# A decoder block with product-key experts: splits, one-hots and stored tiles issued earlier, and a second of four one-hots on VectorE

## The chip, the cores and the metric

The kernel runs on one core of one Trainium2 chip (trn2). The metric is the device time of one execution in microseconds (us). The kernel before took 1837.16 us, the median of three runs that lie between 1837.00 and 1837.48 us. Where engines are named: PE is TensorE, ACT is ScalarE, DVE is VectorE, POOL is GpSimd, and SP is the queue of SyncE, from which most transfers are started.

## The reference

One decoder block: 512 tokens of width 1024 behind 16 meta tokens, a mixer of stick-breaking attention and gated linear attention, then a mixer of 16384 single-neuron experts, of which each of 8 heads picks 16 by product keys, and a last norm. The change lies wholly in the second mixer:

```python
def peer_ffn(hn, w_peer_q, sub_keys1, sub_keys2, expert_u, expert_v):
    q = (t @ w_peer_q).reshape(T, PEER_HEADS, 2, PEER_HALF)
    s1 = jnp.einsum('thd,hkd->thk', q[:, :, 0], sub_keys1)
    s2 = jnp.einsum('thd,hkd->thk', q[:, :, 1], sub_keys2)
    v1, i1 = lax.top_k(s1, PEER_TOPK)
    v2, i2 = lax.top_k(s2, PEER_TOPK)
    cand = (v1[..., :, None] + v2[..., None, :])      # 256 sums per head
    sc, pos = lax.top_k(cand, PEER_TOPK)
    eidx = ...                                        # i1 * 128 + i2 of the 16 best
    gates = jax.nn.softmax(sc, axis=-1)
    act = jax.nn.gelu(jnp.einsum('nkd,nd->nk', expert_u[e], xt), approximate=False)
    return jnp.einsum('nk,nkd->nd', g * act, expert_v[e])
```

Everything is float32.

## The kernel before, in words

The 512 tokens are four blocks of 128. For block 3 (`GATHER`) the kernel fetches the chosen rows of `expert_u` and `expert_v` by indirect transfers. For blocks 0 to 2 (`DENSE`, 384 tokens) it multiplies with all 16384 experts and weights each activation by a matrix of gates that is zero where an expert wasn't chosen.

The experts are handled in 128 rows of 128. A **U row** (`u_row`, lines 832 to 842) loads one 512 KB tile `uf` of `expert_ut`, splits it into a high and a low part (`hilo`, line 174: ACT makes `uh` at line 175, DVE makes `ul` at line 176), multiplies both with the split tokens in 24 products `pj` of 128x384 (lines 180 to 182), and takes the Gelu into `ge` on ACT (line 842). A **V row** (`v_operands` and `v_block`, lines 847 to 870) loads a tile of `expert_v` into the same ring of `uf` buffers, splits it, multiplies `ge` with the gates `gt` (DVE, line 859), splits the result into `wh` and `wl`, and adds 18 products of 128x512 into six banks `acc`. Two rows are a **pair** and share one `ge` tile.

The gate matrix has to be made first. `topk(blk)` finds the 16 experts per head on DVE (lines 640 to 718). `spread(blk)` (line 744) then turns the lists of one block into the matrix: for each **group** of four tokens, `B` is a one-hot of the second key (four Abs at line 786 and a Relu at line 787 on ACT, or one comparison at line 781 on DVE), `Am` is the gated one-hot of the first key (POOL, line 789, from `ohu` and `ohl`, which DVE makes once for four groups), four float32 products `sx` join them (line 793, eight TensorE instructions in the profile), and ACT copies the bank into `st` (line 794). After four groups `st` goes to `Gd` in device memory. A block has 32 groups; `B` and `Am` have three buffers each.

The program has three stretches here. In the **look stretch** (lines 892 to 901) a `Queue` holds topk and spread of the blocks in turn; after each U row it writes out as much of them as a budget of 5.04 us (4.2 * 1.2) pays for at the costs they yield, and the finished U rows are stored in `Ad`. This takes 22 pairs. In the **mixed stretch** (lines 913 to 940) the other 42 pairs run through U and V, with the gathered block between them; in the **stored stretch** the 22 stored pairs come back from `Ad` and only have their V rows done. The order in which the code is written is a priority: a scheduler sorts each engine's instructions by it and by when it believes they are ready, and so sets the order on every engine. Each engine, and SP with its transfers, then works strictly in its order.

## Time and profile before

| | us |
|---|---|
| median of 3 runs | 1837.16 |
| the profiled execution, its own time | 1841.8 |
| its span in the trace | 1840.0 |
| look stretch, in the trace | 441 to 902 |
| mixed stretch | 902 to 1600 |
| stored stretch | 1600 to 1816 |

| engine | busy us | share of the span |
|---|---|---|
| PE | 1631.4 | 89% |
| DVE | 1131.6 | 61% |
| ACT | 810.1 | 44% |
| POOL | 503.9 | 27% |

The profiled execution took 1841.8 us, 4.6 us more than the median of the three runs. The share of an engine is an average over stretches that differ much, so the rows below are read stretch by stretch. In a row of instructions, the bracket at its end says how long the engine had stood idle before it and what released it.

### The profile page before, as it was taken

To read this page: it belongs to the slowest core of one execution; us is meant where nothing else is said; L and a number is where in the kernel's file an instruction comes from. 1 tells how busy PE (TensorE), PEld (TensorE's weight loads), DVE (VectorE), ACT (ScalarE), POOL (GpSimd) and SP (SyncE) were. 2 spreads that over 40 slices of the span, in tenths; PEclk is the share of its full clock that TensorE was granted. 3 is DMA by queue.
4 is the path that set the end of the run, shared out by engine and by line. 5 is a ranking of instruction groups with operands and counts; after the bars stand their busy time and mean duration, and the time that the engine had idled before them with its cause. 6 is when DMAs were issued, how large, how long until landed. Compare 5 with 4: busy or idle time off the path is not lost.

```text
span 1840.0 us, 24030 instructions
## 1 busy us (share of the span) xinstructions
PE 1631.4 (89%) x8727; PEld 1421.9 (77%) x8727; DVE 1131.6 (61%) x2367; ACT 810.1 (44%) x1407; POOL 503.9 (27%) x407
## 2 busy tenths in 40 slices
PE   6999989979777777776789999999999999988996
PEld 4864777867766767765778899889988998866885
DVE  4111384545814824915878877877887778767654
ACT  5255463433486486486223333333333333322343
POOL 0013000000231232242245454534543444343000
PEclk8999989989988888888989999999999999989998
DMA  5200211322333333333699999899899899998743
GB/s 172 63 13 12 81 35 58 115 101 94 129 121 141 105 127 132 120 141 121 234 374 308 316 350 307 312 340 321 295 349 324 301 328 332 320 311 295 247 160 114
DMA packets 148310, 373.62 MB, mean 203 GB/s; under 512 B 12736, under 2 KB 65104, under 8 KB 145120
## 3 DMA queue, kind: packets, MB, share of 16 engines
q1 hardware_dynamic: 103552, 200.90, 32.6%
q0 software_dynamic: 36864, 134.23, 20.5%
q10 hardware_dynamic: 7776, 36.97, 5.0%
q8 instruction: 68, 1.11, 0.3%
q14 instruction: 50, 0.41, 0.1%
HBM read 334.01 MB, written 38.01 MB: 202 GB/s over the span
## 4 chain that ended last, share of the span: by engine, by line
PE 67%; DVE 14%; ACT 9%; DMA 6%; issue 3%; POOL 1%; SPq 0%; ACTq 0%; DVEq 0%; POOLq 0%
PE pj L180 10%; PE pj L182 10%; PE pj L181 10%; PE acc L182 8%; PE acc L180 8%; PE acc L181 8%; PE sx L793 4%; ACT st L794 3%; DMA ge<-Ad 3%; ACT B L786 2%; DVE ul L176 2%; ACT B L787 1%; DVE sc L692 1%; DMA uf<-expert_v 1%; DVE iu L649 1%
## 5 line engine op out<-in xcount | busy, mean ns | idle before, releaser
L175 ACT ACTIVATE uh<-uf 128x1024 fp32r<-128x1024 f32 x256 | 269.2, 1053 | 367.9 <-PE pj L181 300.5
L176 DVE TENSOR_TENSOR ul<-uf,uh 128x1024 fp32r<-128x1024 f32 x256 | 315.4, 1233 | 166.6 <-ACT uh L175 164.4
L182 PE MATMUL pj<-xDh,ul 128*128 128x384 f32 x1024 | 352.5, 344 | 35.1 <-DVE ul L176 35.1
L180 PE MATMUL pj<-xDh,uh 128*128 128x384 f32 x1024 | 354.3, 346 | 9.3 <-ACT ge L842 8.0
L181 PE MATMUL pj<-xDl,uh 128*128 128x384 f32 x1024 | 350.7, 342 | 0.0
L182 PE MATMUL acc<-uh,wl 128*128 128x512 f32 x768 | 308.0, 401 | 15.8 <-DVE wl L176 15.8
L180 PE MATMUL acc<-uh,wh 128*128 128x512 f32 x768 | 307.3, 400 | 12.6 <-ACT wh L175 12.6
L181 PE MATMUL acc<-ul,wh 128*128 128x512 f32 x768 | 307.5, 400 | 0.0
L789 POOL TENSOR_TENSOR Am<-ohu,ohl 128x512 f32<-128x512 f32 x96 | 111.6, 1172 | 547.9 <-ACT B L786 306.4
L724 POOL DMA_INDIRECT gu<-expert_u,idx x128 | 181.5, 1418 | 250.5 <-DVE gu L731 116.7
L724 POOL DMA_INDIRECT gu<-expert_v,idx x128 | 184.3, 1440 | 231.8 <-DVE y L742 160.0
L182 PEld LDWEIGHTS pj<-xDh,ul 128*128 128x128 f32 x1024 | 197.4, 193 | 40.0 <-DVE ul L176 39.8
L175 ACT ACTIVATE wh<-ge 128x384 fp32r<-128x384 f32 x128 | 67.1, 525 | 348.6 <-PE acc L181 328.2
L180 PEld LDWEIGHTS pj<-xDh,uh 128*128 128x128 f32 x1024 | 197.7, 193 | 14.4 <-ACT ge L842 10.7
L181 PEld LDWEIGHTS pj<-xDl,uh 128*128 128x128 f32 x1024 | 197.7, 193 | 1.7
L793 PE MATMUL sx<-Am,B 128*128 128x128 f32 x768 | 127.2, 328 | 71.2 <-ACT B L787 65.5
L182 PEld LDWEIGHTS acc<-uh,wl 128*128 128x128 f32 x768 | 146.7, 191 | 54.1 <-DVE wl L176 19.2
L180 PEld LDWEIGHTS acc<-uh,wh 128*128 128x128 f32 x768 | 146.8, 191 | 46.5 <-ACT wh L175 13.2
L793 PEld LDWEIGHTS sx<-Am,B 128*128 128x128 f32 x768 | 117.2, 237 | 83.2 <-issue 43.0
L181 PEld LDWEIGHTS acc<-ul,wh 128*128 128x128 f32 x768 | 146.5, 191 | 33.8
L742 DVE SCALAR_TENSOR_TENSOR y<-gu,act,y 128x1024 f32<-128x1024 f32 x128 | 163.8, 1280 | 1.2
L731 DVE SCALAR_TENSOR_TENSOR gu<-gu,xn 128x1024 f32<-128x1024 f32 x128 | 153.9, 1219 | 9.0 <-DMA gu<-expert_u,idx 9.0
(314 smaller groups left out, 2210.3 us busy)
## 6 DMA issues: line engine op xcount, KB each, us to landing
uf<-expert_ut SPq DMA_DIRECT2D x128, 512.0 KB
uf<-expert_v SPq DMA_DIRECT2D x128, 512.0 KB
gt<-Gd SPq DMA_DIRECT2D x17, 1536.0 KB
Gd<-st ACTq DMA_DIRECT2D x24, 1024.0 KB
wf<-w_in SPq DMA_DIRECT2D x24, 512.0 KB
Ad<-ge ACTq DMA_DIRECT2D x22, 384.0 KB
ge<-Ad SPq DMA_DIRECT2D x22, 384.0 KB
wf<-w_out SPq DMA_DIRECT2D x8, 512.0 KB
```

What stands on the lines that cost most here:

```text
L175: A.activation(hi, src, AF.Copy)
L176: V.tensor_tensor(lo, src, hi.bitcast(F32), op=OP.subtract)
L180: T.matmul(outp, lh, rh, start=first, stop=False, skip_group_check=True)
L181: T.matmul(outp, lh, rl, start=False, stop=False, skip_group_check=True)
L182: T.matmul(outp, ll, rh, start=False, stop=last, skip_group_check=True)
L724: P.indirect_dma_start(out=u, out_offset=None, in_=d[table], in_offset=bass.IndirectOffsetOnAxis(ap=col, axis=0))
L731: V.scalar_tensor_tensor(u, u, 1.0, xns[blk], op0=OP.mult, op1=OP.mult, accum_out=acts[blk][:, k:k + 1]))
L742: V.scalar_tensor_tensor(y, u, acts[blk][:, k:k + 1], y, op0=OP.mult, op1=OP.add))
L786: A.activation(B[:, j], io128, AF.Abs, bias=nT[:, t:t + 1])
L789: P.tensor_tensor(Am.rearrange("p t (u l) -> p t u l", l=8), ohu[:, l_].unsqueeze(3).to_broadcast([128, 4, 16, 8]), ohl[:, l_].unsqueeze(2 ...
L793: T.matmul(p[:, j * 128:(j + 1) * 128], B[:, j], Am[:, j], start=True, stop=True)
L794: A.activation(st[:, :, t4 * 4:t4 * 4 + 4].rearrange("p i t -> p t i"), p.rearrange("p (t i) -> p t i", t=4), AF.Copy)
```

## The change

Four edits, all in the code after `spread`'s set-up:

- In `spread`, `make(n)` writes out the one-hots of group n (and, for the first of four groups, `ohu` and `ohl`). It is called for two groups before the first product and then for group n + 2 ahead of the products of group n. The queue is handed control once per group at a cost of 0.8 (before: 0.5 or 1.0 per group and 1.2 per four groups).
- `B` is compared on DVE for every second group (16 of 32 per block), before for every fourth (8 of 32).
- `u_row` is cut in two: `u_split` (load and split) and `u_row` (products and Gelu). The split of the next row is written ahead of the products of the current one; in the mixed and stored stretches the same goes for U and V rows alike, through a list `items`.
- `weights_in` loads the gate tile `gt` of a group of eight rows one group ahead, and `fetch` loads a stored pair three pairs ahead of its use (before: one).

The look stretch now takes 20 pairs, because the costs that `spread` yields add up to 27.1 per block (before 31.1); so 44 pairs run in the mixed stretch and 20 in the stored one.

```diff
--- before.py
+++ after.py
@@ -761,40 +761,55 @@
         yield 1.5
         sh = [128, 4, 128]
         io4 = io128.unsqueeze(1).to_broadcast(sh)
-        for tb in range(128 // TT):
...
-            yield 1.2
-            for t4 in range(TT // 4):
...
-                if t4 == TT // 4 - 1:
-                    V.tensor_tensor(B, io4, iT[:, 1, c_].unsqueeze(2).to_broadcast(sh), op=OP.is_equal)
...
-                yield 1.0 if t4 == TT // 4 - 1 else 0.5
-            nc.scalar.dma_start(Gd[128 // TT * DENSE.index(blk) + tb], st)
+        n4 = TT // 4
+        made, oh, sts = {}, {}, {}
+
+        def make(n):
+            tb, t4 = divmod(n, n4)
+            if t4 == 0:
+                tc_ = slice(tb * TT, (tb + 1) * TT)
...
+                oh[tb] = ohu, ohl
+            ohu, ohl = oh[tb]
+            l_ = slice(t4 * 4, t4 * 4 + 4)
+            B = bp.tile(sh, F32, name="B", bufs=nb)
+            if t4 % 2:
+                V.tensor_tensor(B, io4, iT[:, 1, n * 4:n * 4 + 4].unsqueeze(2).to_broadcast(sh), op=OP.is_equal)
+            else:
+
+                for t in range(4):
+                    A.activation(B[:, t], io128, AF.Abs, bias=nT[:, n * 4 + t:n * 4 + t + 1])
+                A.activation(B, B, AF.Relu, scale=-1.0, bias=1.0)
...
+            made[n] = B, Am
+
+        for n in range(nb - 1):
+            make(n)
+        for n in range(128 // 4):
+            if n + nb - 1 < 128 // 4:
+                make(n + nb - 1)
+            tb, t4 = divmod(n, n4)
+            if t4 == 0:
+                sts[tb] = bp.tile([128, 128, TT], F32, name="st", bufs=2)
+            st = sts[tb]
+            B, Am = made.pop(n)
+            p = bank("sx")
+            for t in range(4):
+                T.matmul(p[:, t * 128:(t + 1) * 128], B[:, t], Am[:, t], start=True, stop=True)
+            A.activation(st[:, :, t4 * 4:t4 * 4 + 4].rearrange("p i t -> p t i"),
+                         p.rearrange("p (t i) -> p t i", t=4), AF.Copy)
+            if t4 == n4 - 1:
+                nc.scalar.dma_start(Gd[128 // TT * DENSE.index(blk) + tb], st)
+            yield 0.8
 
 
     front()
@@ -829,34 +844,38 @@
 
     tks = {b: topk(b) for b in range(NB)}
 
-    def u_row(i1, dst):
+    def u_split(i1):
 
         uf = du.tile([128, KT, 128], F32, name="uf", bufs=UF)
         uh = du.tile([128, KT, 128], F32R, name="uh", bufs=UH)
         ul = du.tile([128, KT, 128], F32R, name="ul", bufs=UH)
         nc.sync.dma_start(uf, d["expert_ut"][i1])
         hilo(uh, ul, uf)
+        return uh, ul
+
+    def u_row(sp, dst):
+
+        uh, ul = sp
         pu = pj()[:, :DT]
         for kt in range(KT):
             mm3(pu, (uh[:, kt], ul[:, kt]), (xDh[:, kt, :DT], xDl[:, kt, :DT]), kt == 0, kt == KT - 1)
         A.activation(dst, pu, AF.Gelu)
 
-    gt = None
-    gti = -1
+    gts = {}
+
+    def weights_in(g_):
+        if g_ not in gts:
+            gt = gts[g_] = dp.tile([128, TB, IC, TT], F32, name="gt", bufs=2)
+            nc.sync.dma_start(gt, Gd[:, :, g_ * IC:g_ * IC + IC, :].rearrange("a p i t -> p a i t"))
 
     def v_operands(i1, ge):
-        nonlocal gt, gti
         vf = du.tile([128, D], F32, name="uf", bufs=UF)
         nc.sync.dma_start(vf, d["expert_v"][i1 * 128:(i1 + 1) * 128, :])
         vh = du.tile([128, D], F32R, name="uh", bufs=UH)
         vl = du.tile([128, D], F32R, name="ul", bufs=UH)
         hilo(vh, vl, vf)
-        if i1 // IC != gti:
-            gti = i1 // IC
-            gt = dp.tile([128, TB, IC, TT], F32, name="gt", bufs=2)
-            nc.sync.dma_start(gt, Gd[:, :, gti * IC:gti * IC + IC, :].rearrange("a p i t -> p a i t"))
         g3 = ge.rearrange("p (a t) -> p a t", t=TT)
-        V.tensor_tensor(g3, g3, gt[:, :, i1 % IC, :], op=OP.mult)
+        V.tensor_tensor(g3, g3, gts[i1 // IC][:, :, i1 % IC, :], op=OP.mult)
         wh = dp.tile([128, DT], F32R, name="wh2", bufs=2)
         wl = dp.tile([128, DT], F32R, name="wl2", bufs=2)
         hilo(wh, wl, ge)
...
-    while look.jobs and np_ < NK // 2:
+    ahead = u_split(0)
+    while look.jobs and np_ < NK // 2 - 1:
         gp = pair()
         for i in range(2):
-            u_row(2 * np_ + i, gp[:, i])
+            sp, ahead = ahead, u_split(2 * np_ + i + 1)
+            u_row(sp, gp[:, i])
             look.run(4.2 * RATES[0])
         nc.scalar.dma_start(Ad[np_], gp)
         np_ += 1
@@ -911,32 +932,60 @@
 
 
     order = list(range(np_, NK // 2)) + list(range(np_))
-    pairs = {}
+    groups = [p_ * 2 // IC for p_ in order]
+    pairs, left = {}, []
+
+    def u_item(p_, i):
+        if i == 0:
+            pairs[p_] = pair()
+        gp = pairs[p_]
+        sp = ahead if (p_, i) == (np_, 0) else u_split(2 * p_ + i)
+        return lambda: u_row(sp, gp[:, i])
+
+    def v_item(n, i):
+        p_ = order[n]
+        if i == 0:
+            weights_in(groups[n])
+            later = [g_ for g_ in groups[n:] if g_ != groups[n]]
+            if n + 1 < len(order) and groups[n + 1] != groups[n]:
+                gts_done.append(groups[n])
+            elif later and later[0] not in gts and (n == 0 or groups[n - 1] == groups[n]):
+                weights_in(later[0])
+            if n + 3 < len(order) and order[n + 3] < np_:
+                fetch(order[n + 3])
+        ops = v_operands(2 * p_ + i, pairs[p_][:, i])
+        if i == 1:
+            pairs.pop(p_)
+            if gts_done:
+                gts.pop(gts_done.pop())
+        if n == len(order) - 1:
+            left.append(ops)
+            return lambda: None
+
+        def run():
+            for b in range(ND):
+                for j in range(2):
+                    v_block(ops, b, j, n == 0 and i == 0, False)
+        return run
 
     def fetch(p_):
...
+        pairs[p_] = pair()
+        nc.sync.dma_start(pairs[p_], Ad[p_])
+
+    gts_done = []
+    items = [(u_item, np_, 0), (u_item, np_, 1)]
+    for n in range(len(order)):
+        if n + 1 < len(order) and order[n + 1] >= np_:
+            items += [(u_item, order[n + 1], 0), (u_item, order[n + 1], 1)]
+        items += [(v_item, n, 0), (v_item, n, 1)]
+    run = None
+    for f, a, b in items:
+        nxt = f(a, b)
+        if run is not None:
+            run()
+            rows.run(4.15 * RATES[1])
+        run = nxt
+    run()
     for _ in gen:
         pass
     for b in range(ND):
```

**ACT, in the middle of the first spread.** Before, about four groups of ACT's work are ordered like this (line 786 is Abs, 787 Relu, 794 the copy into `st`, 842 the Gelu of a U row; a count stands behind the size):

```order
L786 ACTIVATE B<-io_80,nT 128x128 x5
L787 ACTIVATE B<-B 128x512
L786 ACTIVATE B<-io_80,nT 128x128 x3
L842 ACTIVATE ge<-pj 128x384
L794 ACTIVATE st<-sx 128x4x128
L787 ACTIVATE B<-B 128x512
L786 ACTIVATE B<-io_80,nT 128x128 x4
L794 ACTIVATE st<-sx 128x4x128
L787 ACTIVATE B<-B 128x512
L794 ACTIVATE st<-sx 128x4x128
L786 ACTIVATE B<-io_80,nT 128x128
L797 DMA Gd<-st 128x2048
```

Now, in the same place, lines 787, 788 and 808 being Abs, Relu and the copy:

```order
L787 ACTIVATE B<-io_80,nT 128x128 x4
L808 ACTIVATE st<-sx 128x4x128
L788 ACTIVATE B<-B 128x512
L808 ACTIVATE st<-sx 128x4x128
L787 ACTIVATE B<-io_80,nT 128x128
L811 DMA Gd<-st 128x2048
L787 ACTIVATE B<-io_80,nT 128x128 x3
L808 ACTIVATE st<-sx 128x4x128
L788 ACTIVATE B<-B 128x512
L808 ACTIVATE st<-sx 128x4x128
```

Two copies now stand against each set of four Abs and one Relu, in a pattern that repeats every two groups, where before four copies stood against three sets; the Abs of a later group stand ahead of a copy in both.

**SP, from the look stretch into the mixed one.** Before, `uf` loads of the U side (line 837) and the V side (850), the gate tiles (857) and the gathered block's start (876):

```order
L850 DMA uf<-expert_v 128x1024
L876 DMA y<-hd 128x1024
L857 DMA gt<-Gd 128x24x128
L850 DMA uf<-expert_v 128x1024
L837 DMA uf<-expert_ut 128x1024 x2
L850 DMA uf<-expert_v 128x1024
L857 DMA gt<-Gd 128x24x128
L850 DMA uf<-expert_v 128x1024
L837 DMA uf<-expert_ut 128x1024 x2
L850 DMA uf<-expert_v 128x1024
L857 DMA gt<-Gd 128x24x128
L850 DMA uf<-expert_v 128x1024
```

Now (lines 852, 873, 869 and 895):

```order
L873 DMA uf<-expert_v 128x1024 x2
L852 DMA uf<-expert_ut 128x1024
L895 DMA y<-hd 128x1024
L869 DMA gt<-Gd 128x24x128 x2
L852 DMA uf<-expert_ut 128x1024
L873 DMA uf<-expert_v 128x1024 x2
L852 DMA uf<-expert_ut 128x1024 x2
L873 DMA uf<-expert_v 128x1024 x2
L852 DMA uf<-expert_ut 128x1024 x2
L873 DMA uf<-expert_v 128x1024 x2
L852 DMA uf<-expert_ut 128x1024
L869 DMA gt<-Gd 128x24x128
```

The first two gate tiles now stand together ahead of the third V load, and the third gate tile comes after eight V loads instead of five.

## Rows read from the trace of the kernel before

**Rows 1.** The head of the page.

```profile
span 1840.0 us, 24030 instructions
```

**Rows 2.** Busy time of each engine by stretches: the stretch, its length, busy us and instruction count of PE, of PE's weight loads, of DVE, ACT and POOL, the granted clock of TensorE, the share of the DMA engines, GB/s. In the order of the rows: topk of block 0, spread of block 0, topk 1, spread 1, topk 2, spread 2, topk 3, then the mixed and the stored stretch.

```profile
441.00:488.00 47.00, 37.90 (x188) 35.00 (x189) 47.00 (x248) 15.77 (x20) 0.00 (x0) 0.93 0.38 122
488.00:582.00 94.00, 67.84 (x419) 63.20 (x418) 24.55 (x48) 78.66 (x167) 36.98 (x32) 0.85 0.37 138
582.00:628.00 46.00, 33.33 (x156) 31.76 (x155) 45.39 (x254) 12.25 (x17) 0.00 (x0) 0.81 0.26 90
628.00:721.00 93.00, 68.61 (x423) 64.05 (x421) 26.39 (x46) 77.89 (x165) 36.79 (x32) 0.85 0.36 136
721.00:767.00 46.00, 36.48 (x191) 34.70 (x187) 45.99 (x253) 14.57 (x21) 0.00 (x0) 0.89 0.34 118
767.00:854.00 87.00, 65.73 (x423) 61.46 (x424) 27.08 (x48) 76.23 (x164) 37.82 (x32) 0.88 0.34 131
854.00:902.00 48.00, 32.58 (x166) 30.98 (x165) 47.99 (x257) 15.31 (x22) 0.46 (x1) 0.82 0.40 134
...
902.00:1600.00 698.00, 685.43 (x3429) 618.15 (x3429) 545.55 (x693) 238.97 (x335) 328.66 (x234) 0.99 0.93 326
1600.00:1816.00 216.00, 200.16 (x832) 159.49 (x831) 134.74 (x172) 72.36 (x101) 36.64 (x22) 0.96 0.72 242
```

**Rows 3.** The groups of instructions of the first spread (488 to 582 us): line, engine, operation, out<-in, sizes and count, then busy us, mean ns of one, and the idle time before them with what ended it.

```profile
L793 PE MATMUL sx<-Am,B 128*128 128x128 f32 x256 | 43.1, 332 | 25.9 <-ACT B L787 22.7 <-POOL Am L789 3.1
L789 POOL TENSOR_TENSOR Am<-ohu,ohl 128x512 f32<-128x512 f32 x32 | 37.0, 1163 | 347.0 <-ACT B L786 306.4 <-issue 20.8 <-PE sx L793 19.4
L794 ACT ACTIVATE st<-sx 128x512 f32<-128x512 f32 x32 | 33.2, 1046 | 11.9 <-PE sx L793 11.7
L786 ACT ACTIVATE B<-io,nT 128x128 f32<-128x128 f32 x96 | 30.5, 387 | 0.0
...
L787 ACT ACTIVATE B<-B 128x512 f32<-128x512 f32 x24 | 15.0, 624 | 0.1
...
L176 DVE TENSOR_TENSOR ul<-uf,uh 128x1024 fp32r<-128x1024 f32 x8 | 10.2, 1282 | 11.6 <-ACT uh L175 11.6
L175 ACT ACTIVATE uh<-uf 128x1024 fp32r<-128x1024 f32 x6 | 6.2, 1046 | 3.5 <-PE pj L181 3.5
L781 DVE TENSOR_TENSOR B<-io,iT 128x512 f32<-128x512 f32 x8 | 6.1, 762 | 19.2 <-PE sx L793 19.2
...
L842 ACT ACTIVATE ge<-pj 128x384 f32<-128x384 f32 x6 | 2.9, 486 | 2.3 <-PE pj L182 2.3
```

**Rows 4.** Instructions in order of time in the same spread, all engines: start, us, engine, line, what, count, and the idle time before.

```profile
528.06 5.46 PE L793 MATMUL sx<-Am,B 128*128 128x128 f32 x24 [2.85 <-ACT B L787]
...
533.56 1.03 ACT L794 ACTIVATE st<-sx 128x512 f32<-128x512 f32 x1 [0.22 <-PE sx L793]
...
534.39 0.62 ACT L787 ACTIVATE B<-B 128x512 f32<-128x512 f32 x1
...
537.16 1.24 ACT L786 ACTIVATE B<-io,nT 128x128 f32<-128x128 f32 x4
...
538.30 0.61 ACT L787 ACTIVATE B<-B 128x512 f32<-128x512 f32 x1
...
538.82 0.97 ACT L786 ACTIVATE B<-io,nT 128x128 f32<-128x128 f32 x3
539.06 5.17 PE L793 MATMUL sx<-Am,B 128*128 128x128 f32 x24 [2.77 <-ACT B L787]
```

**Rows 5.** Two stretches of four us there (columns as in rows 2), and the products of two groups from the first of them.

```profile
520.00:524.00 4.00, 2.02 (x16) 1.86 (x16) 0.00 (x0) 3.85 (x9) 2.29 (x3) 1.00 0.00 0
...
528.00:532.00 4.00, 3.94 (x18) 3.97 (x19) 0.02 (x1) 3.27 (x9) 1.10 (x2) 0.50 0.30 119
...
521.31 2.02 PE L793 MATMUL sx<-Am,B 128*128 128x128 f32 x16 [1.64 <-ACT B L787]
```

**Rows 6.** The same DVE instruction (line 771) twice in the first spread, and the POOL instruction beside the first.

```profile
497.81 1.09 POOL L789 TENSOR_TENSOR Am<-ohu,ohl 128x512 f32<-128x512 f32 x1 [0.32 <-DVE ohl L773]
497.89 1.15 DVE L771 TENSOR_TENSOR ohl<-io,iT 128x128 f32<-128x128 f32 x1
...
505.09 0.28 DVE L771 TENSOR_TENSOR ohl<-io,iT 128x128 f32<-128x128 f32 x1
```

**Rows 7.** Who waited for whom in the look stretch (440 to 902 us): total us, times, longest.

```profile
PE sx L793 <- ACT B L787: 65.5, 44, 2.9
...
PE pj L182 <- DVE ul L176: 35.1, 15, 12.3
```

**Rows 8.** The first product of a V row, of the U row behind it, and of that row's 25th, in the mixed stretch, in order of time.

```profile
1203.24 0.40 PE L180 MATMUL acc<-uh,wh 128*128 128x512 f32 x1
...
1207.44 0.34 PE L180 MATMUL pj<-xDh,uh 128*128 128x384 f32 x1
...
1211.60 0.34 PE L180 MATMUL pj<-xDh,uh 128*128 128x384 f32 x1
```

**Rows 9.** The products before which PE stood idle longest at the start of the mixed stretch.

```profile
919.86 0.80 PE L180 MATMUL acc<-uh,wh 128*128 128x512 f32 x1 [5.68 <-ACT wh L175]
946.58 0.79 PE L180 MATMUL acc<-uh,wh 128*128 128x512 f32 x1 [6.89 <-ACT wh L175]
```

**Rows 10.** A row of the waits between 1590 and 1815 us, columns as in rows 7.

```profile
DVE ge L859 <- DMA ge<-Ad: 48.4, 18, 9.4
```

More of the change, by code (lines that the diff above doesn't have):

```diff
@@ L763, in spread @@
         io4 = io128.unsqueeze(1).to_broadcast(sh)
-        for tb in range(128 // TT):
-            st = bp.tile([128, 128, TT], F32, name="st", bufs=2)
-            tc_ = slice(tb * TT, (tb + 1) * TT)
-            ohu = bp.tile([128, TT, 16], F32, name="ohu", bufs=2)
-            V.tensor_tensor(ohu, io128[:, :16].unsqueeze(1).to_broadcast([128, TT, 16]),
-                            iT[:, 0, tc_].unsqueeze(2).to_broadcast([128, TT, 16]), op=OP.is_equal)
-            ohl = bp.tile([128, TT, 8], F32, name="ohl", bufs=2)
-            V.tensor_tensor(ohl, io128[:, :8].unsqueeze(1).to_broadcast([128, TT, 8]),
-                            iT[:, 3, tc_].unsqueeze(2).to_broadcast([128, TT, 8]), op=OP.is_equal)
-            V.tensor_tensor(ohl, ohl, iT[:, 2, tc_].unsqueeze(2).to_broadcast([128, TT, 8]), op=OP.mult)
-            yield 1.2
-            for t4 in range(TT // 4):
-                p = bank("sx")
-                c_ = slice(tb * TT + t4 * 4, tb * TT + t4 * 4 + 4)
-                l_ = slice(t4 * 4, t4 * 4 + 4)
-                B = bp.tile(sh, F32, name="B", bufs=nb)
-                if t4 == TT // 4 - 1:
-                    V.tensor_tensor(B, io4, iT[:, 1, c_].unsqueeze(2).to_broadcast(sh), op=OP.is_equal)
-                else:
-                    for j in range(4):
-                        t = tb * TT + t4 * 4 + j
-                        A.activation(B[:, j], io128, AF.Abs, bias=nT[:, t:t + 1])
-                    A.activation(B, B, AF.Relu, scale=-1.0, bias=1.0)
-                Am = bp.tile(sh, F32, name="Am", bufs=nb)
-                P.tensor_tensor(Am.rearrange("p t (u l) -> p t u l", l=8),
-                                ohu[:, l_].unsqueeze(3).to_broadcast([128, 4, 16, 8]),
-                                ohl[:, l_].unsqueeze(2).to_broadcast([128, 4, 16, 8]), op=OP.mult)
-                for j in range(4):
-                    T.matmul(p[:, j * 128:(j + 1) * 128], B[:, j], Am[:, j], start=True, stop=True)
-                A.activation(st[:, :, t4 * 4:t4 * 4 + 4].rearrange("p i t -> p t i"),
-                             p.rearrange("p (t i) -> p t i", t=4), AF.Copy)
-                yield 1.0 if t4 == TT // 4 - 1 else 0.5
-            nc.scalar.dma_start(Gd[128 // TT * DENSE.index(blk) + tb], st)
@@ L913, in build @@
     order = list(range(np_, NK // 2)) + list(range(np_))
-    pairs = {}
-    def fetch(p_):
-        gp = pairs[p_] = pair()
-        if p_ >= np_:
-            for i in range(2):
-                u_row(2 * p_ + i, gp[:, i])
-                rows.run(4.2 * RATES[1])
-        else:
-            nc.sync.dma_start(gp, Ad[p_])
-    left = []
-    fetch(order[0])
-    for n, p_ in enumerate(order):
-        if n + 1 < NK // 2:
-            fetch(order[n + 1])
-        gp = pairs.pop(p_)
-        for i in range(2):
-            ops = v_operands(2 * p_ + i, gp[:, i])
-            if n < NK // 2 - 1:
-                for b in range(ND):
-                    for j in range(2):
-                        v_block(ops, b, j, n == 0 and i == 0, False)
-            else:
-                left.append(ops)
-            rows.run(4.1 * RATES[1])
+    groups = [p_ * 2 // IC for p_ in order]
```

11 lines of the change are left out of this document (added).

## The prediction, made before the changed kernel was run

> **What bounds the kernel now.** I read the busy time by stretches first, then the groups of one spread, then single instructions there. The stretches [rows 2] show where PE is not kept busy. In the mixed stretch it is busy for 685 of 698 us at a granted clock of 0.99: nothing in front of PE can give more than 13 us there. The stored stretch has 16 us of idle PE in 216. The look stretch is the loose one: 461 us, and it has two faces. In the four topk parts (47 + 46 + 46 + 48 = 187 us) DVE is busy all the time (47.0 of 47, 45.4 of 46, 46.0 of 46, 48.0 of 48) while PE runs dry; the wait named there is PE for DVE's `ul`, 35.1 us over the look stretch [rows 7]. In the three spreads (94 + 93 + 87 = 274 us, mean 91.3) no engine is full: ACT has 76 to 79 us, PE 66 to 69, DVE 25 to 27, POOL 37 to 38 [rows 2].
>
> The groups of one spread say which loop that is [rows 3, 7]. PE's `sx` products wait for ACT's `B` (22.7 us in this spread, 65.5 us in all), ACT's copy waits for the products (11.7 us), DVE's `B` and POOL's `Am` wait for the products to give a buffer back (19.2 and 19.4 us). The order of time shows one turn [rows 4]: three groups at once on PE, then ACT catches up, and PE is idle for 2.77 us until the next Relu. From the start of one such run (528.06) to the next (539.06) four groups take 11.0 us.
>
> **Part 1, the one-hots two groups ahead and half of them on DVE.** From the starts of successive instructions, ACT needs 538.30 - 537.16 = 1.14 us for four Abs, 538.82 - 538.30 = 0.52 for a Relu, and 534.39 - 533.56 = 0.83 for a copy [rows 4]. Before, a spread costs ACT 24 x (1.14 + 0.52) + 32 x 0.83 = 39.8 + 26.6 = 66.4 us, plus the U rows' 6.2 + 2.9 [rows 3]: 75.5 of the 94 us; 18.5 us are lost to waiting. After, 16 sets of Abs and Relu and the same copies make 26.6 + 26.6 = 53.1; the new order has 4 splits (1.05) and 5 Gelus (0.49) in the first spread, 6.6 us: 59.7 us. That is the floor that ACT sets. PE's floor at full clock: two groups took 2.02 us [rows 5], so 32 groups take 32.3 us; the new order has 105, 125 and 105 U products in the three spreads, 112 on average, at 4.16 / 24 = 0.173 us each [rows 8], 19.4 us: 51.7 us. At half clock three groups took 5.46 us [rows 4]; the granted clock in that stretch was 0.50, 1.2 GHz, after stretches with PE idle for half of the time and more [rows 5]. So the same work there would be 32 x 1.82 + 112 x 0.347 = 97 us. In the spreads of before the clock averages 0.85 to 0.88 [rows 2], and a PE that waits less should not lose more of it.
>
> DVE takes over 8 comparisons per spread at 0.76 us [rows 3], 6.1 us. They hide behind ACT while DVE is busy for 25 of 94 us; if that cover were gone they would cost up to 6 us a spread. POOL's work is the same.
>
> Between ACT's floor (60 us plus about 6 us from the end of topk to the first group) and no gain at all (91) I choose 75: the 18.5 us lost before shrink because `B` is there when PE asks, but three or four blocks of 24 U products (4.2 us each) stand between the groups in PE's new order, and while they run, ACT can do one set and one split (1.66 + 1.54 = 3.2 us) before its next copy, queued in order, waits for PE; and some half-clock stretches stay. Queued behind such a copy are the Abs of the group after next, so the two groups in hand are what PE then lives on. Term: 3 x (75 - 91.3) = -49 us; bounds 3 x (66 - 91.3) = -76 and 3 x (97 - 91.3) = +17.
>
> A rule that speaks against this part is in the Trainium skill, "SBUF — State Buffer", section "Who interferes with whom": a DVE instruction with two SBUF inputs and a GpSimd instruction that reads SBUF shut each other out for a whole instruction. The trace agrees: the same comparison took 1.15 us when it began 0.08 us after an `Am`, and 0.28 us alone [rows 6]. Every comparison moved to DVE has two such inputs. By that rule the second rival below has its cause.
>
> **Part 2, the splits one product ahead.** In topk DVE's own list sets the length, so a split ahead fills PE but shortens nothing: the new order has 10, 6, 6 and 8 `ul` splits in the four topk parts against 9, 5, 6 and 8. Two more at 1.2 us (the mean is 1.28 in a spread, with POOL beside it [rows 3]) make +2.4 us. In the mixed stretch PE's order is the same alternation of 24 U and 18 V products and PE is already at 0.98; I take 0, bounds -5 and +5 (a split behind the gathers' work on DVE).
>
> **Part 3, fewer pairs in the look stretch.** The costs that the spreads yield fall from 31.1 to 27.1, so the look stretch covers 40 U rows, not 44. The 4 rows go to the mixed stretch, where PE is the bound: 4 x (1211.60 - 1207.44) = 4 x 4.16 = +16.6 us [rows 8]. In the topk parts such rows were nearly free, in the spreads not, which is why the gain of part 1 counts fewer U products. V work is the same: 128 rows.
>
> **Part 4, gate tiles and stored pairs ahead.** At the start of the mixed stretch PE stands idle for 5.7 and 6.9 us [rows 9], waiting behind transfers; the DMA engines are busy for 0.93 of that stretch [rows 2]. Two gate tiles now go first and the third one is due three V loads later. I take -2 us, bounds -12 and +8 (the two first tiles push the first V loads back). In the stored stretch DVE waits 48.4 us for `ge` from `Ad` [rows 10] and PE loses 16 us [rows 2]. The loads are now written three pairs ahead, but five `ge` buffers and DVE's order, which places the multiplication by the gates about four pairs ahead of its use in both versions, are as before. I take -3, bounds -15 and +5. SP works in order: a `ge` load waiting for its buffer holds up the V loads behind it, which DVE's splits need next; that is the upper bound.
>
> **The sum.** -49 + 2.4 + 16.6 - 2 - 3 = -35 us on the profiled execution: 1841.8 - 35 = 1806.8 us (the span of before was 1840.0 [rows 1], so about 1805). The median of the three runs lies 4.6 us below the profiled one, so the prediction is 1837.2 - 35 = 1802 us, 1.9% faster.
>
> **Rivals.** First, ACT's floor is reached: spreads of 66 us, and the two waits of part 4 halve (-14): -76 + 19 - 14 = -71, 1766 us. For it: ACT's lost time is nearly all named as waits on PE. Against it: no spread of before comes near its floor.
>
> Second, a loop stays, only with other members: two `Am` (2 x 1.16), one DVE `B` (0.76) and the products of two groups (2.02) one after another, because with three buffers each waits for the other. That is 5.1 us per two groups, where before four took 11.0; 16 x 5.1 = 82, and a few us of start: 84 us a spread. 3 x (84 - 91.3) = -22, +19 - 5 = -8: 1829 us. For it: the waits of DVE and POOL on `sx` [rows 3] and the lock [rows 6]. Against it: `Am` and `B` are now made two groups early.
>
> Third, slower: PE at half clock in the spreads. Its work then takes 97 us there: +17 + 19 - 5 = +31, 1868 us. It decides from the point where the spreads stay above 91.3 - 14 / 3 = 86.6 us, that is a mean granted clock below 51.7 / 86.6 = 0.60 with PE never waiting. For it: the half-clock runs of rows 4. Against it: the mean of 0.85.
>
> Fourth, the change does little of what it says: the scheduler already put Abs of a later group ahead of a copy, so looking ahead in the code adds nothing, and ACT's saved 13 us a spread turn into waiting: +14 us of parts 2 to 4 against some -15, about 1836 us.
>
> **How the numbers follow.** A measurement of this kernel can tell about 0.2% (4 us) from no change. Forecast 58% (its own range 1786 to 1818), first rival 16%, second 14%, third 6%, fourth 6%. To leave no more than 2 in 10 out, the range runs from 1768 to 1832: it holds the forecast, the second rival and the upper part of the first. Faster: the forecast, the first rival and most of the second, 86%; the same 6%; slower: the third and part of the fourth, 8%.
>
> **What would show it.** Right: three spreads of 70 to 80 us, with PE's wait for ACT's `B` far below 65.5 us; topk parts still 46 to 50 us with DVE full; the look stretch at about 415 us; the mixed stretch longer by some 15 us with PE at 0.98 or more. Wrong in part 1: spreads above 84 us, with either POOL and DVE waiting for each other or a clock near 0.6. Wrong in part 4: PE idle at the start of the mixed stretch well above 12.6 us. The prediction as a whole is wrong if the topk parts shrink as well (DVE then was not their bound), or if the mixed stretch grows by more than 25 us.

## The result and the profile after

The changed kernel took 1786.6 us, the median of four runs (1785.0 to 1787.9), beside 1837.3 for the kernel before (median of four): a ratio of 0.9721 with a 95% interval of 0.9704 to 0.9737. That is 50.7 us less, 2.8%; forecast were 35 us less, 1802 us, with a range of 1768 to 1832.

The span of its profiled execution, which took 1785.0 us, is 1783.3 us, where before it was 1840.0 [rows 1]. Busy time by stretches, columns as in [rows 2], in the order of the rows: topk of block 0, spread 0, topk 1, spread 1, topk 2, spread 2, topk 3, the mixed and the stored stretch.

```profile
434.90:486.20 51.30, 43.14 (x218) 40.67 (x215) 51.09 (x259) 20.05 (x26) 0.00 (x0) 0.90 0.35 119
486.20:557.50 71.30, 55.31 (x400) 52.01 (x399) 37.64 (x53) 62.37 (x124) 42.46 (x32) 0.98 0.43 158
557.50:604.10 46.60, 35.08 (x189) 33.39 (x188) 46.54 (x254) 14.41 (x21) 0.00 (x0) 0.93 0.38 132
604.10:673.00 68.90, 56.08 (x418) 53.51 (x418) 36.10 (x54) 62.38 (x124) 43.22 (x32) 1.00 0.43 159
673.00:719.70 46.70, 27.12 (x134) 25.90 (x133) 46.54 (x254) 13.37 (x18) 0.00 (x0) 0.78 0.31 112
719.70:789.70 70.00, 56.14 (x399) 53.29 (x398) 36.62 (x52) 62.30 (x124) 42.41 (x32) 0.95 0.43 163
789.70:836.20 46.50, 32.29 (x149) 30.69 (x149) 46.50 (x255) 13.16 (x18) 0.00 (x0) 0.78 0.31 107
836.20:1565.50 729.30, 714.74 (x3569) 644.98 (x3568) 569.12 (x720) 249.18 (x350) 345.34 (x243) 0.99 0.92 323
1565.50:1768.00 202.50, 189.68 (x793) 150.25 (x791) 118.58 (x161) 69.65 (x100) 20.81 (x14) 0.98 0.65 217
```

The three spreads fell from 94, 93 and 87 us to 71.3, 68.9 and 70.0. ACT is now busy for 62.4 of some 70 us, and the granted clock in them rose from 0.85 to 0.88 [rows 2] to 0.95 to 1.00. The topk parts did not move, with DVE still full. Cut at the same events (first MAX8 of topk, the last block's list of experts, the last Gelu of a U row, the last `acc` product), the two traces differ by -60.8 us in the look stretch, +29.1 in the mixed and -21.5 in the stored one, and -3.5 ahead of and behind all this, where nothing was changed: -56.7 us together. The profiled run of before lies 4.5 us above its median and that of after 1.6 below, so the traces show about 6 us more than the medians do. By the same cuts the three spreads together are 63 us shorter and the four topk parts together 2.2 us longer.

The groups of the second spread (604.1 to 673), columns as in [rows 3]:

```profile
L790 POOL TENSOR_TENSOR Am<-ohu,ohl 128x512 f32<-128x512 f32 x32 | 43.2, 1371 | 74.5 <-DVE ohl L777 59.5 <-PE sx L807 15.1
L808 ACT ACTIVATE st<-sx 128x512 f32<-128x512 f32 x32 | 33.3, 1048 | 4.2 <-PE sx L807 4.1
L807 PE MATMUL sx<-Am,B 128*128 128x128 f32 x256 | 32.7, 279 | 12.8 <-ACT B L788 7.2 <-DVE B L783 3.2 <-POOL Am L790 2.3
...
L783 DVE TENSOR_TENSOR B<-io,iT 128x512 f32<-128x512 f32 x16 | 13.6, 853 | 20.9 <-PE sx L807 20.9
```

PE's `sx` products take 32.7 us, which is 32 groups at full clock (the prediction's 32.3), where before they took 43.1: in this spread the runs at half clock are gone. ACT's copies wait 4.2 us for PE instead of 11.9. (The rows of before are those of the first spread; over all three the `sx` products took 43.1, 43.5 and 40.6 us before and take 34.4, 32.7 and 35.6 now.) `Am` takes 1.37 us (1.16 before) and `B` on DVE 0.85 (0.76): POOL and DVE get more into each other's way, but both have time to spare.

The turn of the loop in order of time, as in [rows 4]:

```profile
640.61 1.04 ACT L808 ACTIVATE st<-sx 128x512 f32<-128x512 f32 x1
...
640.86 2.02 PE L807 MATMUL sx<-Am,B 128*128 128x128 f32 x16 [0.77 <-ACT B L788]
...
644.28 1.04 ACT L808 ACTIVATE st<-sx 128x512 f32<-128x512 f32 x1
...
644.52 2.02 PE L807 MATMUL sx<-Am,B 128*128 128x128 f32 x16 [1.64 <-ACT B L788]
```

PE now takes two groups at a time, at full clock, and comes back after 3.66 us. ACT's work for two groups, from the prediction's durations, is 1.14 + 0.52 + 2 x 0.83 = 3.32 us, and its own turn, from the copy at 640.61 to the one at 644.28, takes 3.67, in which it also starts the transfer of `st` (0.33): so ACT sets the turn. Four groups took 11.0 us before and take 7.3 now.

Who waited for whom in the look stretch (435 to 837), as in [rows 7]:

```profile
DVE B L783 <- PE sx L807: 64.6, 33, 3.5
...
PE pj L182 <- DVE ul L176: 42.1, 13, 14.7
...
PE sx L807 <- ACT B L788: 27.3, 20, 2.5
```

PE's wait for ACT's `B` went from 65.5 to 27.3 us. DVE's long wait for PE costs nothing: there it is ahead of the products and waits for one of the three buffers of `B`. At the start of the mixed stretch PE stands idle longest before these two products (compare [rows 9]):

```profile
849.79 0.69 PE L182 MATMUL pj<-xDh,ul 128*128 128x384 f32 x1 [5.22 <-DVE ul L176]
872.55 0.69 PE L180 MATMUL pj<-xDh,uh 128*128 128x384 f32 x1 [8.12 <-ACT uh L175]
```

The wait for stored tiles between 1565 and 1768 us (compare [rows 10]):

```profile
DVE ge L878 <- DMA ge<-Ad: 50.4, 17, 5.4
```

So PE's two waits at the start of the mixed stretch add up to 13.3 us, against 12.6 before, and DVE's wait for the stored `ge` is 50.4 us, against 48.4. The loads ahead removed neither.

### The profile page after: what moved, and what is told of

Same layout as the page of the kernel before. It is cut to its first block, busy times and chain, and to the rows that moved or that the text cites. A ratio compares the mean times of both kernels' runs of the same rounds, so it can differ in the third digit from the quotient of the medians.

```text
span 1783.3 us, 23943 instructions
## 1 busy us (share of the span) xinstructions
PE 1601.9 (90%) x8727; PEld 1400.2 (79%) x8727; DVE 1168.9 (66%) x2391; ACT 769.0 (43%) x1287; POOL 520.9 (29%) x407
## 4 chain that ended last, share of the span: by engine, by line
PE 66%; DVE 17%; ACT 7%; DMA 6%; issue 2%; POOL 0%; SPq 0%; ACTq 0%; DVEq 0%; POOLq 0%
PE pj L182 11%; PE pj L180 11%; PE pj L181 11%; PE acc L181 8%; PE acc L182 8%; PE acc L180 8%; DMA ge<-Ad 3%; ACT st L808 3%; DVE ul L176 3%; DMA uf<-expert_ut 2%; PE sx L807 2%; ACT B L787 1%; DVE sc L692 1%; DVE sc L651 1%; DVE iu L649 1%
## 5 line engine op out<-in xcount | busy, mean ns | idle before, releaser
L790 POOL TENSOR_TENSOR Am<-ohu,ohl 128x512 f32<-128x512 f32 x96 | 128.1, 1355 | 469.8 <-DVE ohl L777 423.8
L180 PEld LDWEIGHTS pj<-xDh,uh 128*128 128x128 f32 x1024 | 199.0, 194 | 21.1 <-ACT uh L175 12.6
L182 PEld LDWEIGHTS acc<-uh,wl 128*128 128x128 f32 x768 | 145.1, 189 | 48.1 <-DVE wl L176 13.7
L176 DVE TENSOR_TENSOR wl<-wf,wh 128x1024 fp32r<-128x1024 f32 (+1 forms) x42 | 49.8, 1186 | 149.7 <-ACT wh L175 149.7
L807 PE MATMUL sx<-Am,B 128*128 128x128 f32 x768 | 102.7, 288 | 41.6 <-ACT B L788 27.3
```

The costliest lines, as they stand in the source:

```text
L176: V.tensor_tensor(lo, src, hi.bitcast(F32), op=OP.subtract)
L180: T.matmul(outp, lh, rh, start=first, stop=False, skip_group_check=True)
L182: T.matmul(outp, ll, rh, start=False, stop=last, skip_group_check=True)
L790: P.tensor_tensor(Am.rearrange("p t (u l) -> p t u l", l=8), ohu[:, l_].unsqueeze(3).to_broadcast([128, 4, 16, 8]), ohl[:, l_].unsqueeze(2 ...
L807: T.matmul(p[:, t * 128:(t + 1) * 128], B[:, t], Am[:, t], start=True, stop=True)
```

## The experiments

Each kernel was timed beside the kernel before on the same chip; ratios are to that one, with 95% intervals. Two kernels that were not timed beside each other are compared by their ratios.

### The offload alone

The kernel before with one condition changed, so that DVE compares every second group; nothing is made ahead:

```diff
-                if t4 == TT // 4 - 1:
+                if t4 % 2:
                     V.tensor_tensor(B, io4, iT[:, 1, c_]...
```

> The kernel before, with one edit: B is compared on DVE for every second group (16 of 32 per block); the one-hots stand where they stood, right ahead of their products, and all else is as before. Theory A (looking ahead is what opened the loop; ACT's load is only the floor under it): a turn of four groups loses one set of Abs and Relu (1.66 us) from its 11.0 us at most, often less because ACT then waits for the products; spreads of 80 to 92 us (91.3 before), 1800 to 1837 us, and half-clock products in the spreads stay (granted clock there below 0.92). Theory B (ACT's load was the bound, looking ahead matters little): spreads near 70 us as in the changed kernel, 1775 to 1790 us.

Measured: 1795.9 us, 0.9755 (0.9719 to 0.9792). Its three spreads, columns as in [rows 2]:

```profile
485.80:563.10 77.30, 62.20 (x416) 58.68 (x414) 36.46 (x55) 65.13 (x126) 42.78 (x32) 0.91 0.42 158
608.50:683.50 75.00, 60.55 (x418) 56.17 (x416) 39.20 (x55) 65.14 (x126) 41.75 (x32) 0.95 0.44 164
730.40:808.00 77.60, 64.66 (x447) 61.34 (x447) 41.86 (x57) 67.02 (x129) 43.90 (x32) 0.96 0.43 161
```

The mean is 76.6 us and the time 1795.9, both between the two theories. ACT's busy time fell by 11.8 us (77.6 to 65.8) and the rest of the spread, length less ACT, from 13.7 to 10.9. The one line brings 45 us by its ratio, some four fifths of what the whole spread brings below (54), and the clock rises with it.

### The one-hots ahead alone

The kernel before with the changed spread, but DVE comparing every fourth group as before, and the yields set so that 22 pairs stay in the look stretch (the edit against the changed spread):

```diff
-            if t4 % 2:
+            if t4 == n4 - 1:
                 V.tensor_tensor(B, io4, ...
...
-            yield 0.8
+            yield 0.925
```

> The kernel before, with the one-hots written two groups ahead of their products, but B on DVE only for every fourth group as before; the costs that spread yields are set to 31.1 per block, so the look stretch keeps its 22 pairs. Theory A: the spread comes down to ACT's floor for this split of the work, 66.4 + 9.1 = 75.5 us, and some 6 us of start: 79 to 84 us instead of 91.3, 1800 to 1815 us, ACT busy for over 90% of a spread. Theory B: ACT's load is the same as before, so the spreads stay within 3 us of 91 and the time within 10 us of before.

Measured: 1813.6 us, 0.986 (0.9837 to 0.9883). Its three spreads:

```profile
487.10:569.80 82.70, 66.22 (x419) 61.41 (x418) 24.92 (x48) 77.52 (x167) 37.08 (x32) 0.88 0.42 159
615.20:698.30 83.10, 65.53 (x421) 60.73 (x420) 27.64 (x46) 77.40 (x167) 36.97 (x32) 0.90 0.42 160
745.00:824.30 79.30, 61.53 (x390) 56.97 (x389) 26.43 (x47) 75.38 (x164) 37.34 (x32) 0.87 0.38 144
```

A mean of 81.7 us with ACT busy for 76.8, as theory A had it: here the other 4.9 us are all that is lost. Looking ahead hardly takes work off ACT, it takes ACT's waiting away (13.7 to 4.9); the offload mostly does the reverse.

### The whole spread, and the number of pairs

Three kernels separate the spread from what surrounds it: the changed spread in the kernel before with 22 pairs; the changed kernel with 22 pairs (yield 0.925); and the changed spread in the kernel before with 20 pairs. Further down the changed kernel has its splits or its loads undone.

> The kernel before with the changed spread alone (both edits of it), the costs that it yields set to 31.1 per block so that the look stretch keeps its 22 pairs; splits, gate tiles and stored pairs as before. If the spreads are the whole gain (part 1): three spreads of 70 to 76 us and 1775 to 1792 us, as low as the changed kernel or lower, since no U row moves into the mixed stretch. If splits, gate tiles or stored pairs ahead carry part of the gain: 1795 us or more.

> The changed kernel with one number changed: spread yields 0.925 per group, 31.1 per block as before, so that 22 pairs and not 20 run in the look stretch. If a U row in the look stretch is nearly free and costs its 4.16 us of PE in the mixed stretch (part 3 of the sum): 4 to 16 us below the changed kernel's 1786.6. If the spreads now have no idle PE to give to a U row, the rows cost the same in either place: within 4 us of 1786.6. If more U products between the groups hold up ACT's copies: above 1790 us.

> The kernel before with the changed spread and its cost of 0.8, so 20 pairs in the look stretch; splits and loads as before. The same with 22 pairs took 1784.9 us; the changed kernel with its loads (gate tiles, stored pairs) undone, which differs from this one by the splits ahead alone, took 1777.7. Theory A (the splits ahead carry these 7 us): 1783 to 1788 us. Theory B (20 pairs carry them: U rows in the look stretch cost there what they cost later or more): 1775 to 1780 us, spreads about 70 us. Theory C (the prediction's part 3: 4 rows moved cost 16.6 us): 1795 to 1802.

| kernel | us | ratio | interval |
|---|---|---|---|
| spread alone, 22 pairs | 1784.9 | 0.9706 | 0.9684 to 0.9728 |
| spread alone, 20 pairs | 1782.4 | 0.9692 | 0.9679 to 0.9706 |
| all of the change, 22 pairs | 1786.1 | 0.9710 | 0.9691 to 0.9730 |
| all of the change (20 pairs) | 1786.6 | 0.9721 | 0.9704 to 0.9737 |

The spread alone is the whole gain. Two pairs more or fewer in the look stretch make no difference that can be measured, with the rest of the change or without it: with 22 pairs the changed kernel's look stretch is 5.4 us longer (406.7 against 401.3) and all that follows 5.6 us shorter. The products of U rows in the look stretch, with 22 pairs and then with 20 (PE, its weight loads, DVE and ACT, counts in brackets):

```profile
437.20:843.95 406.75, 217.24 (x1102) 201.69 (x1103) 0.00 (x0) 21.61 (x45) 0.94 0.40 145
434.90:836.20 401.30, 203.05 (x1018) 189.38 (x1019) 0.00 (x0) 20.15 (x42) 0.91 0.38 140
```

These are 84 products more, 14.5 us of PE's work at 0.173 us each, for 5.4 us: a row in the look stretch costs about a third of its 4.16 us. What follows doesn't get shorter by those 14.5 us either. The stored stretch with 22 pairs (columns as in [rows 2]):

```profile
1543.20:1769.80 226.60, 207.93 (x859) 164.35 (x857) 138.49 (x182) 74.27 (x107) 37.12 (x24) 0.96 0.69 235
```

PE is idle for 18.7 us of it, with 20 pairs for 12.8 of 202.5. So by these two traces the rows are cheap in the look stretch, and most of what they save later is lost again to waiting.

### The splits ahead, undone

In the changed kernel each split is written next to its own products again:

```diff
...
-            sp, ahead = ahead, u_split(2 * np_ + i + 1)
-            u_row(sp, gp[:, i])
+            u_row(u_split(2 * np_ + i), gp[:, i])
...
-        nxt = f(a, b)
-        if run is not None:
-            run()
-            rows.run(4.15 * RATES[1])
-        run = nxt
+        f(a, b)()
+        rows.run(4.15 * RATES[1])
```

> The changed kernel with each split written next to its own products again, in the look stretch and behind it; nothing else is undone. Theory A (the splits ahead bring nothing: DVE's list sets the topk parts, PE is the bound of the mixed stretch, and the scheduler orders splits by when their tile is there): total within 4 us of the changed kernel, topk parts 46 to 51 us. Theory B (the splits ahead keep PE fed): total 10 us or more longer, PE's wait for DVE's ul in the look stretch clearly above 42 us, idle PE in the mixed stretch above 11 us.

Measured: 1786.1 us, 0.9715 (0.9703 to 0.9728), theory A. With the loads undone as well, though, the same step looks worth something: the next kernel and "spread alone, 20 pairs" differ by the splits ahead, the list that goes with them, and a gate tile's load that is written ahead of its V load instead of behind it, and stand at 0.9664 (0.9646 to 0.9681) and 0.9692 (0.9679 to 0.9706). That is 5 us with intervals that just touch; it isn't settled.

### The loads ahead, undone

In the changed kernel the gate tiles are loaded at their first use and the stored pairs one pair ahead; in a second kernel only the gate tiles' edit is taken back:

```diff
-            elif later and later[0] not in gts and (n == 0 or groups[n - 1] == groups[n]):
-                weights_in(later[0])
-            if n + 3 < len(order) and order[n + 3] < np_:
-                fetch(order[n + 3])
+            if n + 1 < len(order) and order[n + 1] < np_:
+                fetch(order[n + 1])
```

> The changed kernel with the gate tiles loaded at their first use and the stored pairs one pair ahead, as before; nothing else is undone. Theory A (part 4 of the prediction measured nothing: DMA engines are full at the start of the mixed stretch whatever the order is): total within 4 us of the changed kernel, PE idle at the start of the mixed stretch 10 to 16 us, DVE's wait for ge from Ad about 50 us. Theory B (two gate tiles first push V loads back): transition idle below 8 us, total 3 to 8 us shorter. Theory C (loads ahead help): total 5 us or more longer.

> The changed kernel with the gate tiles loaded at their first use, as before the change; the stored pairs stay three pairs ahead. The kernel with both undone took 1777.7 us, 9 less than the changed one. Theory A (the second gate tile, loaded beside the first at the start of the mixed stretch, pushes back the load of the next U row, for which ACT then waited 11.4 us): total 1775 to 1780, PE idle at the start of the mixed stretch about 7 us. Theory B (the stored pairs three ahead are what costs): total 1784 to 1788.

Measured: 1777.7 us, 0.9664 (0.9646 to 0.9681), for both undone, and 1778.5 us, 0.9669 (0.9648 to 0.9690), for the gate tiles alone: theory B of the first, a little beyond its 3 to 8 us, and theory A of the second. So part 4 of the change costs 8 to 9 us by the medians and about 10 by the ratios, and it is the gate tiles' doing. What SP issued at the start of the mixed stretch (start, us, queue, line, what, count), first in the changed kernel:

```profile
833.95 7.81 SPq L869 DMA_DIRECT2D gt<-Gd  x2
841.85 19.48 SPq L852 DMA_DIRECT2D uf<-expert_ut  x1
861.42 1.73 SPq L873 DMA_DIRECT2D uf<-expert_v  x2
```

Then with both undone:

```profile
837.02 0.38 SPq L869 DMA_DIRECT2D gt<-Gd  x1
839.39 4.06 SPq L852 DMA_DIRECT2D uf<-expert_ut  x1
843.54 0.86 SPq L873 DMA_DIRECT2D uf<-expert_v  x2
```

With two gate tiles of 1.5 MB ahead of it, the next U load held SP for 19.48 us instead of 4.06, and the V loads behind it were issued at 861, not 843. ACT waited 11.35 us for that `uf` tile and PE 8.12 us for ACT's `uh`. The stretch from 836 to 900 us in the changed kernel, and then with both undone (columns as in [rows 2]):

```profile
836.00:900.00 64.00, 49.44 (x224) 44.09 (x223) 41.56 (x64) 15.87 (x24) 31.41 (x24) 0.87 0.96 339
```

```profile
836.00:900.00 64.00, 56.37 (x269) 50.85 (x269) 50.08 (x75) 20.18 (x29) 35.00 (x27) 0.92 1.02 372
```

PE is busy for 6.9 us more of these 64. With the gate tiles alone at their use it is busy for 56.4 too; but that trace is of the longest of the kernel's five executions (1787.8 us), so it shows the start and not the whole gain.

Was the `uf` buffer not free yet when SP took 19 us? In the changed kernel:

```profile
835.08 1.21 DVE L176 TENSOR_TENSOR ul<-uf,uh 128x1024 fp32r<-128x1024 f32 x1
...
874.81 1.22 DVE L176 TENSOR_TENSOR ul<-uf,uh 128x1024 fp32r<-128x1024 f32 x1
...
876.06 3.08 SPq L873 DMA_DIRECT2D uf<-expert_v  x2
```

A load that waits for its buffer begins right behind the DVE split that frees it: the one at 876.06 behind the split that ends at 876.03. Each load goes with one split, in order, and counted this way the load at 841.85 goes with the split that ended at 836.29. Its buffer had been free for 5.6 us, so the 19.48 us are the issue's own time behind the two tiles. What held it there the rows don't say.

### All one-hots on DVE

The changed kernel with every `B` compared on DVE (`if True:` for `if t4 % 2:`).

> The changed kernel with B compared on DVE for all 32 groups of a block, so that ACT keeps only the copies, splits and Gelus: 32 x 0.83 + 6.6 = 33 us a spread. Theory lock (DVE's comparison and POOL's Am shut each other out, so their times add): 32 x (1.07 + 0.69) + 8 x 0.99 for ohu and ohl + 6 x 1.22 for the splits = 71.5 us, and 6 us of start: spreads of 75 to 82 us instead of 70, Am and B each at well over their lone 1.07 and 0.69 us in the mean, 1798 to 1825 us. Theory no lock that matters: ACT is far from its floor, PE's 52 us and some start decide, spreads of 55 to 64 us, 1745 to 1770 us.

Measured: 1778.5 us, 0.9688 (0.9662 to 0.9714). Spreads of 65.9, 62.0 and 61.9 us. The groups of the second one (605 to 667):

```profile
L790 POOL TENSOR_TENSOR Am<-ohu,ohl 128x512 f32<-128x512 f32 x32 | 43.1, 1368 | 71.5 <-DVE ohl L777 65.4 <-PE sx L807 5.9
L783 DVE TENSOR_TENSOR B<-io,iT 128x512 f32<-128x512 f32 x32 | 33.8, 1074 | 3.4 <-PE sx L807 3.3
```

Now the two do press on each other: a comparison takes 1.07 us in the mean, where the two in the changed kernel's turn at 641 to 647 us took 0.69 each. Single instructions, and an `Am` of the kernel before with nothing of DVE's beside it, show how:

```profile
639.15 1.15 POOL L790 TENSOR_TENSOR Am<-ohu,ohl 128x512 f32<-128x512 f32 x1
639.30 1.55 DVE L783 TENSOR_TENSOR B<-io,iT 128x512 f32<-128x512 f32 x1
640.26 1.52 POOL L790 TENSOR_TENSOR Am<-ohu,ohl 128x512 f32<-128x512 f32 x1
641.85 0.68 DVE L783 TENSOR_TENSOR B<-io,iT 128x512 f32<-128x512 f32 x1
```

```profile
536.44 1.07 POOL L789 TENSOR_TENSOR Am<-ohu,ohl 128x512 f32<-128x512 f32 x1 [1.70 <-PE sx L793]
```

The `B` that begins under an `Am` (639.30) lasts until 0.55 us after that `Am` has ended, 1.55 us instead of 0.68; the `Am` that begins under this `B` (640.26) lasts until 0.93 us after it, 1.52 instead of 1.07. So the two take turns, with little overlap. Their mean times hold this waiting and can't be added up: 32 x (1.37 + 1.07) = 78 us is more than the spread has. The lone times can, 32 x (1.07 + 0.68) = 56 us, and they fit into the 62. Theory lock had the mechanism, but its 75 to 82 us were too long; whether the turns bound the spread now isn't shown. DVE, its waiting included, is busy for 54.2 of the 62 us.

The spreads are 20 us shorter together, the time only 8 by the medians and 6 by the ratios, whose intervals overlap: the topk parts behind them grew from 46.6 to about 50 us, since the U rows' splits that found no room on DVE in the spreads are done there, where DVE is the bound (9 `ul` splits in each of the last three parts, where the changed kernel has 6 or 7).

### topk of the next block beside the spread

In the changed kernel, the queue takes a piece of `spread(b)` and a piece of `topk(b + 1)` in turns:

```diff
-    look = Queue(tks[0], spread(0), tks[1], spread(1), tks[2], spread(2), tks[3])
+    look = Queue(tks[0], side_by_side(spread(0), tks[1]), side_by_side(spread(1), tks[2]), side_by_side(spread(2), tks[3]))
```

> The changed kernel with the topk of block b + 1 written out in turns with the spread of block b (both in the same queue, the same 20 pairs). Theory stretches (a topk part is bound by DVE, a spread by ACT, and they only add because they stand one after the other): DVE's own sum decides, 191 us of topk and 3 x 37 in the spreads, 300 to 340 us instead of 401 for the look stretch, 1720 to 1750 us, DVE busy for over 85% of it. Rival (DVE works in its order, so the comparisons and splits of a spread stand behind topk instructions and PE and ACT wait for them, or POOL's Am is locked out longer): look stretch of 380 us or more, 1765 us or more.

Measured: 1760.2 us, 0.9569 (0.9540 to 0.9598), faster than both kernels. The look stretch in one row (columns as in [rows 2]), and two of the waits between 773 and 850 us:

```profile
438.00:773.40 335.40, 260.67 (x1626) 249.90 (x1625) 282.99 (x1156) 215.97 (x394) 110.63 (x86) 0.89 0.38 140
```

```profile
DVE ge L878 <- DMA gt<-Gd: 12.7, 1, 12.7
...
PE acc L180 <- ACT wh L175: 12.0, 1, 12.0
```

The stretch is 66 us shorter, as theory stretches had it, the time only 26 (28 by the ratios), between the two theories. In its 335 us 853 products of U rows are on record, in the changed kernel's 401 us 1018: 165 at 0.173 us are 28.5 us of PE's work that now come later, and the first V row waits 12 us, behind DVE's wait for the gates. Two kernels tried to win that back by the order of the loads, one with the second gate tile a pair later, one with all loads as before the change:

> The kernel with topk beside spread, with its second gate tile loaded one pair later (behind the first pair's V loads). In that kernel PE was idle for about 12 of 20 us at the start of the mixed stretch with the DMA engines full. Theory A (the order of these loads decides how long PE waits there): idle there falls to 4 to 8 us and the total is 3 to 8 us below that kernel's 1760. Theory B (the same bytes have to come in any order): the total stays within 3 us of 1760.

> The kernel with topk beside spread (1760 us), with gate tiles and stored pairs loaded as before the change. Theory A (the gain of 9 us that this gave in the changed kernel adds up): 1749 to 1754 us. Theory B (with topk beside spread the start of the mixed stretch is full of transfers in any order, as the second gate tile one pair later showed): 1757 to 1762 us.

Measured: 1759.0 us, 0.9572 (0.9558 to 0.9586), and 1756.9 us, 0.9561 (0.9543 to 0.9578): no difference that the intervals can tell. With all loads as before PE still waits 12.3 us for ACT's `wh` there, behind 13.1 us of DVE's wait for `gt`. My reading is that this is the first gate tile itself, which can't be read before the last spread is written; that was not tried.

## Why the prediction was right, and where it was not

**Part 1, right in its mechanism, too small.** Forecast were 3 x (75 - 91.3) = -49 us; the spreads gave -63 in the trace. ACT's floor was right: 59.7 us forecast, 62.4 us busy. What was mis-sized is the step to 75: "three or four blocks of 24 U products (4.2 us each) stand between the groups ... and some half-clock stretches stay". I kept 15 us of loss, and 7.7 are left (mean length 70.1 less 62.35). Of the half-clock stretches little stayed: the granted clock is 0.95 to 1.00, and in the turn shown PE's two groups take 2.02 us each time. The two edits alone show what each does. The offload takes 11.8 us of work off ACT and leaves 10.9 of loss; looking ahead leaves ACT's work and cuts the loss from 13.7 to 4.9. Alone they shorten a spread by 14.7 and 9.6 us, together by 21.2, less than the sum of 24.3: both go at the same loss, which together they cut to 7.7, not to the 2.1 that their two effects would leave.

**Part 2, as costed in topk.** The topk parts together grew by 2.2 us in the trace (forecast +2.4), and undoing the splits ahead in the changed kernel changes nothing (forecast 0 for the mixed stretch, within 5). Without the loads ahead they may be worth 5 us.

**Part 3, wrong.** The step "The 4 rows go to the mixed stretch, where PE is the bound: ... = +16.6 us" did not come out: 20 or 22 pairs give the same time, in the changed kernel and with the spread alone. In the traces of the changed kernel with 22 and 20 pairs, a row in the look stretch isn't nearly free, it costs a third of its work (5.4 us for 14.5). The larger error is on the other side: without these rows the later stretches are only 5.6 us shorter, as PE waits longer in the stored stretch when that has more pairs to bring back (18.7 us idle against 12.8). Nor did I book the V rows. Two pairs fewer in store move four V rows out of the stored stretch into the mixed one, at the same 4.2 us each; that is 16.8 us of the +29.1 and of the -21.5 in the traces. So my own sign for a prediction that is wrong as a whole, a mixed stretch more than 25 us longer, came about; it was badly set, because it left these V rows out. The later stretches together are 7.6 us longer, where parts 3 and 4 had said 11.6.

**Part 4, wrong sign.** I took -2 and -3 us with bounds up to +8 and +5, and named the mishap as a bound: "the two first tiles push the first V loads back". That is what happened, with the next U load held as well, and it is the value that should have been taken: two runs put it at 8 to 9 us by the medians, about 10 by the ratios. The sign that I had set, idle PE at the start well above 12.6 us, did not show it (13.3): in the kernel without the loads ahead PE is idle for 7.6 us from 836 to 900, in the changed one for 14.6, and only the runs with the edit undone could tell. The stored pairs three ahead changed nothing: DVE's wait for `ge` is 50.4 us where it was 48.4, and taking that edit back as well made no difference.

So -35 came out as -51. By the ratios measured, the change goes like this: the spread -54 us (0.9706; forecast -49), 20 pairs about -3, which the intervals don't tell from nothing (forecast +16.6), the splits ahead about -5, barely resolved (forecast +2.4), and the loads ahead about +10 (forecast -5). The last error goes against the other three and takes off about half of them, so that the time came within 16 us of the forecast is in part luck.

**The rivals.** The first, ACT's floor reached at 66 us a spread and 1766 us, was nearer in the spreads (70) than the forecast, but its halved waits of part 4 didn't come. The second had the right cause and not the effect: a turn of two groups takes 3.66 us, not 5.1. The Trainium skill, "SBUF — State Buffer", section "Who interferes with whom", says that a DVE instruction with two SBUF inputs and one of GpSimd that reads SBUF shut each other out. The traces agree: `Am` went from 1.16 to 1.37 us and `B` from 0.76 to 0.85 in the mean, and in the kernel with all comparisons on DVE single ones take turns (1.55 and 1.52 us). But with half of the comparisons on DVE neither engine is the bound. The third went the other way: a PE that waits less lost less clock, not more. The fourth fell with the spreads at 70 us.

## What to carry to other kernels

Where an engine runs at four fifths of its time in a loop and several engines wait for each other in turn, count its work and its waiting apart: moving work to an idle engine and making operands earlier each take one of the two, and their gains overlap. A load written earlier is not free where its queue works in order: name the load behind it and who waits for that, before booking a gain. When work moves between stretches, book all that goes with it on both sides, and don't take its whole price off the stretch that it leaves: other waits can take its place there. The mean times of two engines that take turns hold each other's waiting; to ask whether their work fits, add up the times that each takes alone.

## What was not expected of the hardware

One line that moves comparisons to DVE raised TensorE's granted clock in the spreads from 0.85 to 0.88 up to 0.91 to 0.96, and the whole change to 0.95 to 1.00, without a change in PE's work: the `sx` products, the same 256 in each spread, went from 42.4 to 34.2 us in the mean, so some 8 us of PE's time a spread had gone to the lower of its two levels. And a U load's issue held SP for 19.48 us behind two tiles of 1.5 MB though its buffer was free, but for 4.06 us behind one.
